# Norm chains with one-tile operands, and where GpSimd's norm products run, in a two-layer decoder trunk

## The chip, the cores and the metric

The kernel runs on one core of a Trainium2 chip. The metric is the device time of one execution in microseconds (us), shown as the median of three runs. PE is TensorE (the matrix engine), DVE is VectorE, ACT is ScalarE, POOL is GpSimd, and SP only issues transfers. Every engine runs its own list of instructions in order and waits on semaphores for the others.

## What is computed

The reference is a trunk of two layers over 512 tokens of width 1024, all in float32:

```python
for l in range(2):
    h = mixing(x)                        # x @ w_in, four kinds of causal heads, RMS norm per head, @ w_out
    x = layernorm(alpha * x + h, ln1_g[l], ln1_b[l])
    m = hier_moe(x)                      # logits -> group (top 1) -> two experts in it, gates
                                         # per expert: (silu(x @ w1) * (x @ w3)) @ w2
    x = layernorm(alpha * x + m, ln2_g[l], ln2_b[l])
def layernorm(x, g, b):
    mu, var = mean(x), mean((x - mu) ** 2)
    return (x - mu) * rsqrt(var + 1e-5) * g + b
```

The mixer has stick-breaking (sb), forgetting (fox), latent (mla) and dilated (d0, d1, d2) heads. There are 16 experts of hidden width 512.

## The kernel before

The 512 tokens are four tiles of 128, one token on a partition. SBUF is handed out by hand: 42 "pages" of 128x1024 floats and 12 small "pg" pages; PSUM is 8 "bank"s; "st" and "nst" are small columns of one value per token. Weights come through one queue on SP, page by page. A weight that isn't used raw is split in two: ACT writes a rounded high part and DVE the rest (`TENSOR_TENSOR page<-page,page 128x1024`, called a lo below), and PE multiplies by both.

All engine orders are written when the kernel is built, by the planner `Plan` (line 88). Each piece of work is a strand that says what it needs (banks, pages, events, an engine). The planner keeps a clock for each engine, costs each instruction, and takes next the strand that could start first, by priority. What it emits is the order of each engine on the chip. All instructions go through one helper, so every row of the trace names line L250, and pieces are told apart by tile names and shapes.

The first norm of a layer (`first_norm`, `first_norm_out`, lines 1464 to 1550) comes after w_out, tile 3 first and tile 0 last. DVE takes the statistics, ACT a first value y of the root, and DVE refines it with `rs_newton` (line 405) and makes m = -mean*y: one tensor_tensor and three scalar_tensor_tensor on 128x1 columns of SBUF. Then ACT writes z = x*y + m. From z, `first_norm_affine` makes z*g + b: POOL for tiles 3, 2, 1 in products of 1024 columns and for the last 384 columns of tile 0; DVE has 640 columns of tile 0 in steps of 160. The logits of the router (`wg`) wait on the same y and m. `route` picks group and experts and writes `asb`, PE counts with it, `posm` gives each token its place in each expert's list, and a list `xidx` comes out; `gslot` are the gates. The expert of rank 0 doesn't wait for a gather: PE selects its rows from SBUF.

The expert loop (line 2263) does for expert e: w1, the first half of w3, then expert e-1's second weights w2 (`hidden_T`, then four quarters), then the rest of w3 and the product silu(h1)*h3. Expert 0 uses its weights raw in float32, others use the split. `use` and `fill` convert weights some places ahead of the one in use.

The second norm of layer 0 (`second_norm`, `second_norm_out`, lines 1591 to 1680) runs from PSUM: statistics and the same chain on DVE, ACT writes z, PE transposes it for the next layer's projections, and POOL makes z*g + b for the residual in two products of 1024 columns per tile and stores it (`xd`). In the last layer ACT writes z from the banks and `affine_by` makes z*g + b on both engines: DVE the first 384, 512, 640, 768 columns of tiles 0 to 3, in steps of 384.

## Time and profile before

| | us |
|---|---|
| median of three runs | 1615.7 (1611.23 to 1615.98) |
| profiled execution, its own time | 1619.65 |
| span of its trace | 1617.7 |
| busy PE, DVE, ACT, POOL | 1436.7, 1099.8, 890.5, 368.7 |

The span has, in this order: attention of layer 0 to about 416 us, its first norm and router to 457, its experts to 765, the second norm and the projections of layer 1 to about 870, the rest of its attention to 1208, its router to 1252, its experts to 1595, and the last norm and the stores to the end. PE is busy most of the time, so what counts is where it stands still and for whom. A bracket at the end of a row of the timeline gives the engine's idle time before that row and what ended it; a row with xN is N instructions that follow each other, and the time is of all of them.

### The profile page before, as it was taken

The numbers are of one execution on the slowest core, as the hardware profiler recorded it, in microseconds if no ns is written. First come the engines' busy times: TensorE is split into PE (matmuls) and PEld (weight loads), VectorE is DVE, ScalarE is ACT, GpSimd is POOL, SyncE is SP. The second block draws the span as 40 slices with busy tenths as digits, with TensorE's granted clock in tenths as the row PEclk, the third lists the DMA queues.
The fourth block names the chain that finished last, engine by engine and source line by source line (L and its number), as shares of the span: only waits on it lengthen the run. The fifth ranks groups of instructions, "written<-read, shape, count | busy, mean of one in ns | idle before, by whom it ended". The sixth has DMA issues, their size and how long they took to land. (4 is left out here: it accounts for less than half of the span.)

```text
span 1617.7 us, 22596 instructions
## 1 busy us (share of the span) xinstructions
PE 1436.7 (89%) x7620; PEld 1164.3 (72%) x7620; DVE 1099.8 (68%) x1967; ACT 890.5 (55%) x1695; POOL 368.7 (23%) x388
## 2 busy tenths in 40 slices
PE   7999989989799999888799998989786999899674
PEld 7988878878666767655699987878666667666453
DVE  4745575476686889977774546654658779898667
ACT  5435454434346888775543534545424477887553
POOL 2511120240412224311421112002204213323002
PEclk9989999999899999988798999989887999999797
DMA  9201211263579999985330102204545799999813
GB/s 266 65 1 41 89 42 40 83 232 143 195 264 319 370 379 356 377 318 173 105 90 23 40 27 92 65 21 134 213 166 195 263 355 382 386 347 385 302 34 130
DMA packets 120700, 303.54 MB, mean 188 GB/s; under 512 B 21982, under 2 KB 45230, under 8 KB 120568
## 3 DMA queue, kind: packets, MB, share of 16 engines
q1 hardware_dynamic: 106936, 269.74, 45.9%
q0 software_dynamic: 12448, 32.11, 7.1%
q8 instruction: 64, 1.05, 0.3%
q14 instruction: 68, 0.56, 0.1%
q10 hardware_dynamic: 1184, 0.08, 0.1%
HBM read 284.14 MB, written 27.33 MB: 193 GB/s over the span
## 5 line engine op out<-in xcount | busy, mean ns | idle before, releaser
L250 PE MATMUL bank<-page,page 128*128 128x512 f32 (+5 forms) x4480 | 983.1, 371 | 62.1 <-DVE page L250 35.0
L250 PEld LDWEIGHTS bank<-page,page 128*128 128x128 f32 (+2 forms) x4480 | 760.6, 203 | 197.9 <-DVE page L250 55.2
L250 DVE TENSOR_TENSOR page<-page,page 128x1024 fp32r<-128x1024 f32 (+3 forms) x470 | 525.7, 1163 | 154.3 <-ACT page L250 140.8
L250 ACT ACTIVATE page<-page 128x1024 fp32r<-128x1024 f32 (+3 forms) x454 | 436.2, 1021 | 49.1 <-DMA page<-in_w_in_dram 11.8
L250 PE MATMUL bank<-page,pg 128*128 128x64 f32 (+1 forms) x1360 | 317.0, 375 | 32.3 <-ACT page L250 14.7
L250 PEld LDWEIGHTS bank<-page,pg 128*128 128x128 f32 x1360 | 227.0, 202 | 115.1 <-issue 37.8
L250 ACT ACTIVATE page<-bank 64x512 fp32r<-64x512 f32 (+8 forms) x255 | 122.1, 506 | 197.1 <-PE bank L250 135.7
L250 ACT ACTIVATE pg<-bank 128x256 f32<-128x256 f32 (+6 forms) x223 | 101.4, 469 | 223.5 <-PE bank L250 221.6
L250 POOL DMA_INDIRECT yd<-page,xidx x30 | 67.5, 2249 | 403.3 <-ACT page L250 165.9
L250 DVE TENSOR_TENSOR page<-bank,page 128x512 fp32r<-128x512 f32 (+4 forms) x142 | 79.9, 599 | 65.9 <-ACT page L250 65.7
L250 POOL TENSOR_TENSOR page<-pg,pg 128x256 f32<-128x256 f32 (+1 forms) x56 | 51.1, 928 | 270.0 <-DVE pg L250 211.5
L250 PE MATMUL bank<-cid,pg 128*128 128x128 f32 (+2 forms) x500 | 84.2, 286 | 29.4 <-ACT pg L250 19.4
L250 POOL TENSOR_TENSOR page<-page,page 128x1024 f32<-128x1024 f32 (+4 forms) x32 | 63.1, 1971 | 153.4 <-ACT page L250 104.7
L250 PE MATMUL bank<-cid,page 128*128 128x128 f32 (+1 forms) x608 | 86.5, 280 | 10.5 <-DVE page L250 5.4
L250 PEld LDWEIGHTS bank<-cid,pg 128*128 128x128 f32 (+2 forms) x500 | 58.7, 147 | 46.2 <-ACT pg L250 25.1
L250 PEld LDWEIGHTS bank<-cid,page 128*128 128x128 f32 (+1 forms) x608 | 71.6, 143 | 24.9 <-DVE page L250 7.7
L250 ACT ACTIVATE pg<-pg 128x256 f32<-128x256 f32 (+5 forms) x146 | 68.6, 477 | 22.3 <-DVE pg L250 18.4
L250 POOL DMA_INDIRECT page<-x1d,xidx x30 | 54.5, 1818 | 42.4 <-DVE e_slots L250 17.9
L250 POOL CAST page<-page 64x512 fp32r<-64x512 f32 x48 | 29.9, 623 | 136.3 <-ACT page L250 102.8
L250 DVE COPY pg<-bank 128x256 f32<-128x256 f32 (+3 forms) x73 | 35.2, 484 | 28.4 <-PE bank L250 28.2
L250 DVE TENSOR_TENSOR pg<-bank,pg 64x512 f32<-64x512 f32 (+6 forms) x81 | 44.8, 559 | 11.9 <-ACT pg L250 10.8
L250 POOL MEMSET page<- 128x1024 f32 (+1 forms) x34 | 44.7, 1319 | 1.8 <-DVE page L250 1.8
(217 smaller groups left out, 974.4 us busy)
## 6 DMA issues: line engine op xcount, KB each, us to landing
page<-in_w_dram SPq DMA_DIRECT2D x396, 512.0 KB, 10.9
page<-in_w_in_dram SPq DMA_DIRECT2D x64, 512.0 KB, 4.1
page<-in_w_out_dram SPq DMA_DIRECT2D x16, 512.0 KB, 4.1
x1d<-page SPq DMA_DIRECT2D x8, 512.0 KB, 2.8
yd<-page SPq DMA_DIRECT2D x8, 512.0 KB, 5.1
page<-yd SPq DMA_DIRECT2D x8, 512.0 KB, 7.0
scr<-pg POOLq DMA_DIRECT2D x16, 132.0 KB, 2.0
pg<-scr POOLq DMA_DIRECT2D x16, 132.0 KB, 4.5
```

What stands on the lines that cost most here:

```text
L250: r = f(*args, **kw)
```

## The change

1. `norm_stats`: `rs_newton` and the m after it are replaced by four tensor_scalar, in which y, v and the mean come as scalars of a partition, so that each has one tensor operand.
2. First norm: tiles 3 and 2 are done on POOL, tiles 1 and 0 on DVE, all in steps of 256 columns (16 products on each engine); DVE's wait for the event `chosen`, which `route` sets when the lists have been started.
3. Second norm of layer 0: POOL's eight products wait for the event `d1q` of the next layer's projections.
4. Last norm: DVE takes (bank - mean)*g from PSUM while ACT makes y, then x*y + b on the first 256, 256, 384, 640 columns; for the rest ACT multiplies by y and POOL adds b. The norm by ACT from the banks is gone.
5. Expert 0's w2 is loaded and used at the end of its own turn, not in expert 1's; expert 1's rows are taken up before its third quarter (`ROWS_AT`).
6. The last expert's w2 is not converted before the product of its hidden layer (`held_at`).
7. The planner lets a DVE tensor_tensor with two SBUF tensors wait for a running POOL tensor_tensor of that kind in its own clocks, which alters the order of other strands.

```diff
+    def newton_1(y, v, t):
+        nc.vector.tensor_scalar(t, y, y, None, op0=OP.mult)
+        nc.vector.tensor_scalar(t, t, -0.5, v, op0=OP.mult, op1=OP.mult)
+        nc.vector.tensor_scalar(y, t, 1.5, y, op0=OP.add, op1=OP.mult)
...
         yield Need(eng="ACT")
         rs_act(y, v)
+        if between:
+            yield from between(mvt[:, 0:1])
         yield Need(eng="DVE")
-        rs_newton(y, v, st(1))
-        nc.vector.scalar_tensor_tensor(m, mvt[:, 0:1], -1.0, y, op0=OP.mult, op1=OP.mult)
+        newton_1(y, v, st(1))
+        nc.vector.tensor_scalar(m, mvt[:, 0:1], -1.0, y, op0=OP.mult, op1=OP.mult)
...
-            plan.spawn(first_norm_affine(nc.gpsimd, t, z, c0, D, D, left), first=1)
-            if c0:
-                plan.spawn(first_norm_affine(nc.vector, t, z, 0, c0, 160, left), first=1)
+            if t in LN1_DVE:                                   # (0, 1)
+                plan.spawn(first_norm_affine(nc.vector, t, z, LN1_STEP, [ev["xT", t], ev["chosen"]]), first=8)
+            else:
+                plan.spawn(first_norm_affine(nc.gpsimd, t, z, LN1_STEP, [ev["xT", t]]), first=1)
...
     def second_norm_out(l, t, z, last, stored):
-        yield Need()
-        affine(t, z, *last.gb, 0, 0)
+        for a in range(0, D, LN2_STEP):                        # 1024
+            for w, op in zip(last.gb, (OP.mult, OP.add)):
+                yield Need(evs=[ev[LN2_AT]], eng="POOL")       # "d1q"
+                c = slice(a, a + LN2_STEP)
+                nc.gpsimd.tensor_tensor(z[:, c], z[:, c], w[:, c], op=op)
...
+                    nc.vector.scalar_tensor_tensor(z[:, c], bs[n], mean, last.gb[0][:, c], op0=OP.subtract, op1=OP.mult)
...
+    def out_sum_1(t, b, cut, y, left):
+        yield Need(eng="DVE")
+        nc.vector.scalar_tensor_tensor(xt[t][:, 0:cut], xt[t][:, 0:cut], y, b[:, 0:cut], op0=OP.mult, op1=OP.add)
+        left()
+    def out_sum_2(t, b, cut, y, left):
+        yield Need(eng="ACT")
+        nc.scalar.activation(xt[t][:, cut:], xt[t][:, cut:], AF.Copy, scale=y)
+        yield Need(eng="POOL")
+        nc.gpsimd.tensor_tensor(xt[t][:, cut:], xt[t][:, cut:], b[:, cut:], op=OP.add)
+        left()
...
-            if e > 0:
+            if e > 1:
                 moe_q[l, e - 1, "w2"] = [block(w2, l, e - 1, q) for q in range(4)]
...
+            if e == 0:
+                moe_q[l, 0, "w2"] = [block(w2, l, 0, q) for q in range(4)]
...
+            if e == 0:
+                ht = hidden_T(prev, "raw" if 0 in RAW_2 else KIND[0])
+                ys = [bank([128, 512]) for _ in range(2)]
+                for j in range(4):
+                    if j == ROWS_AT:                           # 2
+                        next_rows(0)
+                    i = moe_q[l, 0, "w2"][j]
+                    quarter2(ys, ht, use(i), j)
+                    used(i)
+                rel(*ht)
+                scatter(gated(ys, gslot[:, 0:1], KIND[0]), xidx[:, 0:1], SLOTS[0])
+            if e == NE - 1:
+                held_at[0] = moe_q[l, NE - 1, "w2"][3]
+                fill()
...
+                two = "tensor_tensor" in op and ins[0].space != PSUM and ins[-1].space != PSUM
+                if two and eng == "DVE":
+                    for a, b in self.pool_tt:
+                        if a <= start < b:
+                            start = b
```

On DVE, behind the router of layer 0: `xidx` and `gslot` come from the last small matmul, the rows after them rank the experts, and the four 128x1024 rows are los of weights. Before:

```order
L250 TENSOR_SCALAR xidx<-bank_4722 128x16
L250 COPY gslot<-bank_4722 128x16
L250 TENSOR_TENSOR pg_4730<-st_119 128x256
L250 TENSOR_REDUCE st_125<-pg_4730 128x16
L250 TENSOR_TENSOR pg_4730<-st_125,rank_at 128x256
L250 TENSOR_TENSOR pg_4731<-pg_4730,eidx 128x256
L250 TENSOR_REDUCE st_126<-pg_4731 128x16
L250 CAST order<-st_126 128x16
L250 TENSOR_TENSOR pg_4731<-pg_4730,n_slots 128x256
L250 TENSOR_REDUCE e_slots<-pg_4731 128x16
L250 TENSOR_TENSOR page_4752<-page_4180,page_4750 128x1024
L250 TENSOR_TENSOR page_4758<-page_4208,page_4756 128x1024
```

The same place now, from `xidx` on; page_3762 and page_3760 are tiles 1 and 0 of the first norm:

```order
L261 TENSOR_SCALAR xidx<-bank_4711 128x16
L261 COPY gslot<-bank_4711 128x16
L261 TENSOR_TENSOR page_3762<-page_3762,page_4185 128x256
L261 TENSOR_TENSOR pg_4720<-st_119 128x256
L261 TENSOR_TENSOR page_3760<-page_4564,page_4184 128x256
L261 TENSOR_REDUCE st_125<-pg_4720 128x16
L261 TENSOR_TENSOR page_3760<-page_3760,page_4185 128x256
L261 TENSOR_TENSOR pg_4720<-st_125,rank_at 128x256
L261 TENSOR_TENSOR page_3760<-page_4564,page_4184 128x256
L261 TENSOR_TENSOR pg_4721<-pg_4720,eidx 128x256
L261 TENSOR_TENSOR page_3760<-page_3760,page_4185 128x256
L261 TENSOR_REDUCE st_126<-pg_4721 128x16
```

Nine products of the first norm stand among the ranks behind `xidx`; seven more are ahead of it. The eleven rows of `further_table`, three los, and then expert 0's product follow:

```order
L261 TENSOR_TENSOR page_4777<-rk,iota 128x576
L261 TENSOR_TENSOR page_4777<-page_4777,sx_130 128x576
L261 TENSOR_TENSOR page_4780<-page_4777,e_151 128x576
L261 TENSOR_REDUCE extab<-page_4780 128x9
L261 TENSOR_TENSOR page_4780<-page_4777,sx_129 128x576
L261 TENSOR_REDUCE extab<-page_4780 128x9
L261 CAST ntab<-extab 128x9
L261 TENSOR_TENSOR page_4793<-page_4297,page_4791 128x1024
L261 TENSOR_TENSOR page_4797<-page_4299,page_4795 128x1024
L261 TENSOR_TENSOR page_4821<-page_4307,page_4819 128x1024
L261 TENSOR_TENSOR pg_4771<-pg_4771,bank_4786 128x512
```

Here `further_table` (rk, extab, ntab) is a table for experts with many tokens, and pg_4771 is expert 0's silu(h1)*h3. Before, that product stood behind `further_table`, five los and the halves of expert 1's rows, and PE had expert 1's w1 ahead of the first matmul that needs it; now the next matmuls on PE after w3 are those of `hidden_T` on it.

On POOL, at the second norm of layer 0: before, the two products of a tile and its store stand at once behind the loads (page_9407, 9409, 9411 and 9413 are the tiles, page_9509 and 9510 g and b).

```order
L250 TENSOR_TENSOR page_9407<-page_9407,page_9509 128x1024
L250 TENSOR_TENSOR page_9407<-page_9407,page_9510 128x1024
L250 DMA xd_298<-page_9407 128x1024
L250 TENSOR_TENSOR page_9409<-page_9409,page_9509 128x1024
L250 TENSOR_TENSOR page_9409<-page_9409,page_9510 128x1024
L250 DMA xd_298<-page_9409 128x1024
```

Now they stand behind and among the adds that finish the rotary embedding of the dilated heads' q and k (128x256, from pg pages); page_9422, 9424, 9426, 9428 are the tiles:

```order
L261 TENSOR_TENSOR page_10002<-pg_10194,pg_10195 128x256
L261 TENSOR_TENSOR page_9422<-page_9422,page_9524 128x1024
L261 TENSOR_TENSOR page_10206<-pg_10279,pg_10280 128x256
L261 TENSOR_TENSOR page_10206<-pg_10310,pg_10311 128x256
L261 TENSOR_TENSOR page_10206<-pg_10325,pg_10326 128x256
L261 TENSOR_TENSOR page_10206<-pg_10367,pg_10368 128x256
L261 TENSOR_TENSOR page_9424<-page_9424,page_9524 128x1024
L261 TENSOR_TENSOR page_9426<-page_9426,page_9524 128x1024
L261 TENSOR_TENSOR page_9428<-page_9428,page_9524 128x1024
L261 TENSOR_TENSOR page_9422<-page_9422,page_9525 128x1024
L261 CAST page_10499<-page_10499 64x512
```

The products moved from the norm itself to the stage that makes the dilated heads' q and k; three more adds follow among the casts of sb's k.

On DVE, the last rows of the program, the last norm's tiles 2 and 3. Before:

```order
L250 TENSOR_SCALAR st_74<-st_73 128x1
L250 TENSOR_TENSOR page_18732<-page_18732,page_18739 128x384
L250 TENSOR_TENSOR page_18732<-page_18732,page_18739 128x128
L250 TENSOR_TENSOR page_18734<-page_18734,page_18738 128x384
L250 TENSOR_TENSOR page_18734<-page_18734,page_18738 128x256
L250 TENSOR_TENSOR st_75<-nst 128x1
L250 SCALAR_TENSOR_TENSOR st_75<-st_75,st_74 128x1
L250 SCALAR_TENSOR_TENSOR nst<-st_75,nst 128x1
L250 SCALAR_TENSOR_TENSOR nst<-st_73,nst 128x1
L250 TENSOR_TENSOR page_18734<-page_18734,page_18739 128x384
L250 TENSOR_TENSOR page_18734<-page_18734,page_18739 128x256
L250 TENSOR_TENSOR page_18736<-page_18736,page_18738 128x384 x2
```

And now:

```order
L261 TENSOR_SCALAR st_74<-nst 128x1
L261 TENSOR_SCALAR st_74<-st_74,st_71 128x1
L261 TENSOR_SCALAR nst<-st_74,nst 128x1
L261 TENSOR_SCALAR nst<-st_70,nst 128x1
L261 SCALAR_TENSOR_TENSOR page_18766<-bank_18894,st_72,page_18768 128x512
L261 SCALAR_TENSOR_TENSOR page_18764<-page_18764,nst,page_18769 128x384
L261 SCALAR_TENSOR_TENSOR page_18766<-bank_18895,st_72,page_18768 128x512
L261 TENSOR_SCALAR st_75<-nst 128x1
L261 TENSOR_SCALAR st_75<-st_75,st_73 128x1
L261 TENSOR_SCALAR nst<-st_75,nst 128x1
L261 TENSOR_SCALAR nst<-st_72,nst 128x1
L261 SCALAR_TENSOR_TENSOR page_18766<-page_18766,nst,page_18769 128x640
```

The products by g now read a bank and stand ahead of the chain of their tile; one sum of 640 columns is left behind the last chain, where four products of 384 stood.

## Rows read from the trace of the kernel before

**Rows 1.** Page, part 1: busy us (share of the span) xinstructions.

```profile
PE 1436.7 (89%) x7620; PEld 1164.3 (72%) x7620; DVE 1099.8 (68%) x1967; ACT 890.5 (55%) x1695; POOL 368.7 (23%) x388
```

**Rows 2.** Timeline, layer 0's router: start us, us, engine, operation, count [idle before <-releaser].

```profile
419.52 4.82 POOL L250 TENSOR_TENSOR page<-page,page 128x1024 f32<-128x1024 f32 x2 [31.02 <-ACT page L250]
...
422.41 0.15 DVE L250 TENSOR_SCALAR st<-st 128x1 f32<-128x1 f32 x1
...
431.42 3.60 PE L250 MATMUL bank<-wg,page 128*128 128x20 f32 x16
...
433.73 4.77 POOL L250 TENSOR_TENSOR page<-page,page 128x1024 f32<-128x1024 f32 x2 [1.56 <-ACT page L250]
...
434.01 2.09 DVE L250 TENSOR_TENSOR st<-nst 128x1 f32<-128x1 f32 x1 [0.91 <-ACT nst L250]
...
436.33 2.38 DVE L250 SCALAR_TENSOR_TENSOR nst<-st,nst 128x1 f32<-128x1 f32 x2
...
439.65 0.24 DVE L250 TENSOR_TENSOR sel<-lgt,top 128x80 f32<-128x80 f32 x1
...
440.47 0.97 DVE L250 TENSOR_TENSOR sel<-sel,toptmp 128x80 f32<-128x80 f32 x1
...
444.79 0.19 PE L250 MATMUL bank<-asb,tri 128*128 128x16 bf16 x1 [9.77 <-DVE asb L250]
```

**Rows 3.** Timeline, layer 1: from the list to expert 0's product.

```profile
1252.53 10.55 PE L250 MATMUL bank<-page,page 128*128 128x512 f32 x24
1252.71 0.17 DVE L250 TENSOR_SCALAR xidx<-bank 128x16 int32<-128x16 f32 x1 [0.38 <-PE bank L250]
...
1255.86 0.42 DVE L250 TENSOR_REDUCE e_slots<-pg 128x16 f32<-128x256 f32 x1
...
1256.19 4.62 DVE L250 TENSOR_TENSOR page<-page,page 128x1024 fp32r<-128x1024 f32 x4
...
1260.73 0.22 DVE L250 TENSOR_TENSOR sx<-e_slots,c 128x64 f32<-128x64 f32 x1
...
1266.26 0.16 DVE L250 CAST ntab<-extab 128x9 int32<-128x9 f32 x1
```

**Rows 4.** Timeline, last expert of layer 1, then last norm.

```profile
1578.01 1.11 PE L250 MATMUL bank<-cid,pg 128*128 128x128 f32 x4 [3.48 <-DVE pg L250]
...
1595.64 1.48 DVE L250 TENSOR_TENSOR st<-nst 128x1 f32<-128x1 f32 x1
...
1606.69 4.20 DVE L250 TENSOR_TENSOR page<-page,page 128x384 f32<-128x384 f32 x6
```

**Rows 5.** Timeline, second norm of layer 0.

```profile
772.65 1.41 DVE L250 TENSOR_TENSOR st<-nst 128x1 f32<-128x1 f32 x1
...
783.00 5.30 POOL L250 TENSOR_TENSOR page<-page,page 128x1024 f32<-128x1024 f32 x2 [5.67 <-ACT page L250]
783.71 5.67 DVE L250 TENSOR_TENSOR page<-page,page 128x656 fp32r<-128x656 f32 x2 [0.52 <-ACT page L250]
...
811.62 2.93 DVE L250 TENSOR_TENSOR page<-page,page 128x256 fp32r<-128x256 f32 x4
```

**Rows 6.** Waits of PE, 735 to 815: engine, line, waited for: us, times, longest.

```profile
PE bank L250 <- DVE page L250: 13.2, 8, 3.2
```

**Rows 7.** Windows: us, busy (x) of PE, PEld, DVE, ACT, POOL, PEclk, DMA share, GB/s.

```profile
825.00:840.00 15.00, 15.00 (x128) 15.00 (x128) 13.15 (x30) 7.88 (x11) 3.44 (x4) 1.00 0.21 63
1155.00:1185.00 30.00, 17.28 (x74) 12.15 (x72) 22.09 (x92) 13.59 (x49) 4.74 (x8) 0.66 0.30 102
1252.00:1318.00 66.00, 65.61 (x241) 41.47 (x242) 46.09 (x60) 36.88 (x47) 13.43 (x10) 1.00 0.83 296
1320.00:1400.00 80.00, 76.52 (x335) 58.16 (x333) 71.45 (x77) 65.83 (x85) 22.55 (x15) 0.98 1.02 379
```

**Rows 8.** Timeline of PE: ends of the attention of layers 0 and 1.

```profile
352.37 1.12 PE L250 MATMUL bank<-cid,pg 128*128 128x128 f32 x4 [5.60 <-ACT pg L250]
...
1159.38 0.69 PE L250 MATMUL bank<-page,page 128*128 128x128 f32 x2 [4.13 <-DVE page L250]
```

More of the change, by code (lines that the diff above doesn't have):

```diff
@@ L44 @@
 ROWS = 3
+ROWS_AT = 2
 LOOK_AHEAD = (2, 10)
@@ L64 @@
 EX_PAGES = 0
-LN1_DVE = 640
+LN1_DVE = (0, 1)
+LN1_STEP = 256
+LN2_STEP = 1024
+LN2_AT = "d1q"
 XT_DVE = (2, 2)
-OUT_DVE = (384, 512, 640, 768)
-OUT_STEP = 384
+OUT_DVE = (256, 256, 384, 640)
 SPLIT_X = 3
@@ L94, in __init__ @@
             self.books, self.floor, self.moves = {}, {}, []
+            self.pool_tt = deque(maxlen=64)
             self.end = self.now = 0.0
@@ L193, in note @@
             else:
+                two = "tensor_tensor" in op and ins[0].space != PSUM and ins[-1].space != PSUM
[3 more added lines that the diff above has]
+                            start = b
                 end, by = start + self.cost(eng, op, outs, ins), eng
+                if two and eng == "POOL":
+                    self.pool_tt.append((start, end))
                 self.clock[eng] = end
@@ L684, in xT_tile, with norm_stats @@
             rel(b)
-    def norm_stats(t, eps=LN_EPS):
+    def norm_stats(t, eps=LN_EPS, between=None):
         mvt, v = st(2), st(1)
@@ L830, in attention @@
             on(u, NT if U[u].kind == "tok" else 2)
-        for n in ("mla", "forget", "krope", "wfox", "fc"):
+        for n in ("mla", "forget", "krope", "wfox", "fc", "chosen"):
             on(n)
@@ L1603, in second_norm, with centred @@
         yield Need(eng="DVE")
+        z = xt[t]
+        if final:
+            def centred(mean):
+                for n in range(2):
+                    c = slice(n * 512, (n + 1) * 512)
+                    yield Need(eng="DVE")
+                    nc.vector.scalar_tensor_tensor(z[:, c], bs[n], mean, last.gb[0][:, c], op0=OP.subtract, op1=OP.mult)
+                rel(*bs)
+            y, m = yield from norm_stats(t, LN_EPS / ALPHA ** 2, centred)
+            cut = OUT_DVE[t]
+            left = countdown(2, lambda: plan.spawn(second_norm_end(t, last), first=t))
+            plan.spawn(out_sum_2(t, last.gb[1], cut, y, left), first=t)
+            plan.spawn(out_sum_1(t, last.gb[1], cut, y, left), first=t)
+            return
         y, m = yield from norm_stats(t, LN_EPS / ALPHA ** 2)
         yield Need(eng="ACT")
-        z = xt[t]
         for n in range(2):
@@ L1609, in second_norm @@
         rel(*bs)
-        if final:
-            cut = OUT_DVE[t]
-            left = countdown(2, lambda: plan.spawn(second_norm_end(t, last), first=t))
-            for eng, a, b in ((nc.vector, 0, cut), (nc.gpsimd, cut, D)):
-                plan.spawn(affine_by(eng, t, last.gb, a, b, left), first=t)
-            return
         yield Need(pages=1, banks=2)
@@ L1623, in second_norm @@
         plan.spawn(second_norm_out(l, t, z, last, stored[t]))
-    def affine_by(eng, t, gb, c0, c1, left):
-        step = OUT_STEP if eng.name == "DVE" else c1 - c0
-        for w, op in zip(gb, (OP.mult, OP.add)):
-            for a in range(c0, c1, step):
-                yield Need(eng=eng.name)
-                c = slice(a, min(c1, a + step))
-                eng.tensor_tensor(xt[t][:, c], xt[t][:, c], w[:, c], op=op)
+    def out_sum_1(t, b, cut, y, left):
+        yield Need(eng="DVE")
+        nc.vector.scalar_tensor_tensor(xt[t][:, 0:cut], xt[t][:, 0:cut], y, b[:, 0:cut], op0=OP.mult, op1=OP.add)
[5 more added lines that the diff above has]
+        nc.gpsimd.tensor_tensor(xt[t][:, cut:], xt[t][:, cut:], b[:, cut:], op=OP.add)
         left()
@@ L1766, in route @@
             fetched.set()
+            ev["chosen"].set()
             yield dve
@@ L2261, in use_13, with next_rows @@
                 used(i)
+        def next_rows(e):
+            xs_[e + 1] = rows_T(rows.pop(e + 1), KIND[e + 1])
+            if e + ROWS < NE:
+                rows[e + ROWS] = fetch(SLOTS[e + ROWS], xidx[:, e + ROWS:e + ROWS + 1])
         for e in range(NE + 1):
@@ L2278, in trunk @@
                 h3 = bank([128, 512])
-            ht = hidden_T(prev, "raw" if e - 1 in RAW_2 else KIND[e - 1]) if e else None
+            ht = hidden_T(prev, "raw" if e - 1 in RAW_2 else KIND[e - 1]) if e > 1 else None
             if e < NE:
@@ L2283, in trunk @@
                 use_13(e, "w3", h3, range(2))
-            if e:
+            if e > 1:
                 ys = [bank([128, 512]) for _ in range(2)]
@@ L2310, in trunk @@
                 break
-            if e + 1 < NE:
-                xs_[e + 1] = rows_T(rows.pop(e + 1), KIND[e + 1])
-                if e + ROWS < NE:
-                    rows[e + ROWS] = fetch(SLOTS[e + ROWS], xidx[:, e + ROWS:e + ROWS + 1])
+            if 0 < e < NE - 1:
+                next_rows(e)
             if e == EX_RUN:
```

32 lines of the change are left out of this document (11 added, 21 removed).

## The prediction, on record before the changed kernel ran

> **What bounds the kernel now.** I read the page's busy shares first: PE is busy 1436.7 us of the span, far ahead of the others [rows 1]. So the time is PE's work plus the stretches in which PE stands still or runs slowly. The windows show both kinds of stage [rows 7]: with the experts PE is busy 65.61 of 66 us and 76.52 of 80, with the projections of layer 1 15.00 of 15; but at the end of layer 1's attention only 17.28 of 30, at a granted clock of 0.66. What is worth anything are such holes, and I looked at the timeline of each that the change touches.
>
> The hole at the router shows the mechanism on which most of the change turns [rows 2]. A 128x1 product of DVE takes 2.09 us, and the pair behind it 2.38, although each handles one value per partition. Both end where one of POOL's 1024-column products ends: POOL runs 433.73 to 438.50, in two of 2.4 us, and DVE's run ends at 436.10 and 438.71. These DVE instructions have two tensors from SBUF. A tensor_scalar with one, inside POOL's 419.52 to 424.34, took 0.15. So a DVE instruction with two SBUF operands waits for POOL's running product, one with a single SBUF operand does not.
>
> The Trainium skill says the same ("SBUF — State Buffer", section "Who interferes with whom"): DVE's second input comes through ports shared with GpSimd, held for a whole instruction. But the same section, with "VectorE: DVE Perf Modes", section "Mode 2×_2P", also lets tensor_scalar hold the shared pair, where source and destination lie in SBUF and the shape allows it. By that rule the new chains could wait as well; the 0.15 us row speaks against it, for immediate scalars. It is rival 3.
>
> **The change part by part** (against the profiled execution, 1619.65 us with a span of 1617.7; that is 3.95 above the median of 1615.7, and I carry the sum over to the median unchanged).
>
> *Router, both layers.* Four tensor_scalar at 0.15 us are 0.6 for a chain that took from 434.01 to 438.71 [rows 2]: about 4 less. Nothing else is late until PE's last logit matmuls, which end at 431.42 + 3.60 = 435.02 whatever DVE does; the logits need them too, so the choice starts near 435.5 in place of 439.4: -3.9. In the choice itself two products run into POOL's 384-column pair; one shows 0.97 us against 0.24 for its like, so two cost 1.5. In the new order POOL's part is tiles 3 and 2 alone, which come first, and it is idle by then: -1.5. Against that, seven products of tiles 1 and 0 stand ahead of `xidx` on DVE. A 256-column operation is 0.42 us [rows 3], seven are 2.9; DVE waits for PE there in part, so 0 to 2.9, I take +0.9. PE waited 9.77 us for `asb` [rows 2], so all of it is on its path. Sum -4.5 per layer (bounds -1.5 and -5.4), -9 for two; layer 1's rows repeat layer 0's.
>
> *Expert 0's w2 at once.* From `xidx` PE has w1 and w3 of expert 0: 32 float32 matmuls at 10.55/24 = 0.44, so 14.1 us from 1252.53, to 1266.6 [rows 3]. Then comes `hidden_T`, which needs the product. DVE after `xidx` (1252.71): gates and ranks to 1256.28 (3.4), now with nine products of 0.42 between (3.8), `further_table` 1260.73 to 1266.42 (5.7), three los at 4.62/4 = 1.16 (3.5), then the product (about 0.7): 17.1, so it ends near 1269.9. PE waits 3.3, then some 0.6 more for ACT's copy of the transposed tile, which other matmuls covered before. +3.9 per layer (0 if the rows of `further_table` and the los are shorter or start earlier, 6 if the nine also meet POOL), +7.8. Today nothing waits there (65.61 of 66 busy [rows 7]). The rest of the edit moves 16 matmuls and a scatter earlier and is worth nothing: PE does the same work.
>
> *Last expert.* PE waits 3.48 us for a product that stands behind two los of 1.16 [rows 4]. The product goes ahead of them: up to -2.3 per layer; but the los are then late for w2's first quarter. I take -1 each (0 to -2.3): -2.
>
> *Second norm of layer 0.* Seven DVE rows between 772.65 and 811.62 are longer than their kind: 1.41 for 0.15, 5.67 for about 2, 2.93 for about 1.5 [rows 5]; together 12.9 us. In that stretch PE waited 13.2 us for DVE's pages [rows 6]. With POOL idle they go, and ACT's writing of z is next, which already ends a part of PE's waits. I take two thirds: -8 (0 to -11). The chain itself would not wait without POOL, so here the two edits count once.
>
> *The products moved to layer 1's projections.* Eight of 4.82/2 = 2.41 us are 19.3 us of POOL among DVE's adds, los and POOL's own rope adds. DVE is busy 13.15 of 15 us there and PE never waits [rows 7]. A DVE product with two SBUF operands that meets one waits about half of it; the order has slack of a tile or so, so most is hidden: +2 (0 to +19). Their `xd` stores come later, and are read only a layer later. The four tiles and g, b keep six of 42 pages longer, in a stage with a DMA share of 0.21 [rows 7]: nothing.
>
> *Planner.* It reorders the attention of both layers. In layer 0 the end shows one wait of 5.60 us and little else [rows 8]: -2.5 (±3). In layer 1 the last 30 us have 12.7 idle, the largest 4.13 for a DVE page [rows 7, 8], and what runs is slow at 0.66. The new order puts the small sums that merge the dilated heads ahead of fox's scores, as in layer 0, where the hole is smaller, and spreads the filler matmuls over the end in place of one block after it. I take -9: half of the idle and a third of what the clock costs (17.28 us at 0.66 are 11.4 at 1, so 5.9). Bounds -14 and +8.
>
> *The end.* A 128x1 product waits 1.48 us there, and DVE has 4.20 us of sums left in its last row, to 1610.89 [rows 4]. After: one sum of 640 columns (about 0.85) behind the last chain, the products by g from the banks, which PE has finished. By the durations of the shown kinds DVE ends near 1607.1: -3.8 (-2 to -5). POOL's part stays at 256 to 768 columns, one product in place of two.
>
> *Experts between.* PE is the bound to 1318, and later the DMA is as well: a share of 1.02 at 379 GB/s [rows 7]. Loads start as pages come free, pages come free as PE goes on, so an earlier start shifts all of it.
>
> Sum: -2.5 - 9 + 7.8 - 2 - 8 + 2 - 9 - 3.8 = -24.5; 1615.7 - 24.5 = **1591**.
>
> **Rivals.**
>
> 1. *The planner's order brings nothing in layer 1.* Its costs are not the chip's; the holes of 0.4 to 4 us there are chains between ACT, DVE and PE, and any order has them. Then -9 turns to +5 and -2.5 to 0: -8, 1608. For it: the planner also wrote today's order, with this hole. Against it: layer 0 has the better order, and the smaller hole.
> 2. *The loads are the bound.* If the DMA, full from 1318 on, doesn't start earlier, what is gained or lost ahead of the experts is swallowed: -2.5 - 9 + 7.8 - 9 = -12.7 of the sum goes, and 1604 is left. For it: a share of 1.02. Against it: PE is still busy 76.52 of 80.
> 3. *The chains still wait.* If a tensor_scalar with scalars from SBUF columns waits for POOL like the old form, 3.9 per layer is lost: 1599. For it, the form isn't in the trace; against it, the 0.15 us row.
> 4. *The moved products cost more than they did, slower than before.* The place is layer 1's dilated q and k. If PE loses each of the eight in full, that is 19.3 us, and the holes lower the clock as in 1155 to 1185: 30 us of PE work at 0.66 take 15 more. +34 in place of +2: -24.5 + 32 = +7.5, 1623. It decides from 24.5 us above my +2. For it: DVE is the busiest helper there; against it: each product meets one DVE instruction, and PE has matmuls queued.
>
> **How the numbers follow.** My forecast holds with 0.54 (its own range 1578 to 1604), rival 1 with 0.18, rival 2 with 0.12, rival 3 with 0.05, rival 4 with 0.06; 0.05 is left for gains beyond my bounds or a mishap not named. 0.3%, 4.9 us, is about what a measurement of this kernel can tell from no change. Faster by more: 0.54, 0.05, most of rivals 1 and 2 (0.20) and half of the rest: 0.80. Within: the upper ends of rivals 1 and 2: 0.12. Slower: rival 4 and some of the rest: 0.08. The range runs from 1575 (the LN2, planner and end terms at their good bounds lie below) to 1614, which takes in rivals 1 to 3.
>
> **What would show it.** In the changed trace: 128x1 tensor_scalar rows of 0.15 us during POOL's products (rival 3 if they take 1 to 2); PE's wait for `asb` at 5 us in place of 9.8; a new wait of PE for a DVE pg of 3 to 4 us about 14 us after `xidx`; no DVE row over 2 us for one product in the second norm; PE at 15 of 15 still in the projections of layer 1 (rival 4 if it falls below 13); PE over 22 of the last 30 us of layer 1's attention (rival 1 if not). I am wrong above all if the planner's order makes layer 1's end longer, which no row of before can exclude.

## The result, and the profile of the changed kernel

The changed kernel takes 1599.24 us in the median of 6 runs (1596.7 to 1608.6), the kernel before 1614.68 us beside it; the ratio is 0.9915, with a 95% interval of 0.9892 to 0.9938. By the ratio that is 13.7 us faster (the medians lie 15.4 apart), in the range and in the direction of the forecast, and a little over half of its 24.5. One execution of the kernel of experiment 2 took 4735.87 us, three times the others, and is left out of its median as of its ratio. The profiled execution took 1600.47 us with a span of 1598.7, 19.0 less than the span of before. Where these 19.0 come from is read from both traces at the same instructions on DVE: the first aggregate of the statistics of a norm, the list `xidx`, the cast of `xidx` before the last scatter, and the first row on `lat_ss`, the latents' statistics. All stretches are differences of such start times; the end is the span less the last of them.

| stretch, us | before | changed | difference | forecast |
|---|---|---|---|---|
| attention of layer 0, to its first norm | 415.9 | 421.5 | +5.6 | -2.5 |
| router of layer 0, to `xidx` | 41.8 | 36.2 | -5.6 | -4.5 |
| experts of layer 0, to the last scatter | 285.5 | 295.9 | +10.4 | +3.9 |
| last expert, to the second norm | 24.5 | 24.9 | +0.4 | -1 |
| second norm, to `lat_ss` | 55.0 | 42.2 | -12.8 | -8 |
| rest of layer 1's attention | 387.8 | 375.2 | -12.6 | -9 + 2 |
| router of layer 1 | 42.1 | 36.4 | -5.7 | -4.5 |
| experts of layer 1 | 321.3 | 326.3 | +5.0 | +3.9 |
| last expert | 16.2 | 15.6 | -0.6 | -1 |
| last norm and stores | 27.5 | 24.5 | -3.0 | -3.8 |

The sum is near the forecast only because large errors of both signs cancel. The page of the changed kernel, part 1, answers to [rows 1]: PE has 10 us more of busy time for the same 7620 matmuls in a shorter span, DVE 12 less.

```profile
PE 1446.7 (90%) x7620; PEld 1164.4 (73%) x7620; DVE 1087.6 (68%) x1981; ACT 888.1 (56%) x1689; POOL 354.0 (22%) x400
```

The router of layer 0 in the timeline of the changed kernel (start, us, engine, operation, count, idle time before) answers to [rows 2].

```profile
433.69 5.99 POOL L261 TENSOR_TENSOR page<-page,page 128x256 f32<-128x256 f32 x8 [2.36 <-ACT page L261]
...
435.19 0.20 DVE L261 TENSOR_SCALAR st<-nst 128x1 f32<-128x1 f32 x1
...
438.68 0.21 DVE L261 TENSOR_SCALAR st<-nst 128x1 f32<-128x1 f32 x1 [1.49 <-ACT nst L261]
...
440.56 0.24 DVE L261 TENSOR_TENSOR sel<-lgt,top 128x80 f32<-128x80 f32 x1
...
443.75 0.19 PE L261 MATMUL bank<-asb,tri 128*128 128x16 bf16 x1 [3.93 <-DVE asb L261]
```

A tensor_scalar of the new chain takes 0.20 us inside POOL's products of 433.69 to 439.68, where the old form took 2.09. The products of the choice meet no POOL and take 0.24. PE waits 3.93 us for `asb`, not 9.77.

Behind the list of layer 0, the same stretch as [rows 3] (those are of layer 1):

```profile
457.67 0.17 DVE L261 TENSOR_SCALAR xidx<-bank 128x16 int32<-128x16 f32 x1
...
469.07 3.49 DVE L261 TENSOR_TENSOR page<-page,page 128x1024 fp32r<-128x1024 f32 x3
...
472.48 0.68 DVE L261 TENSOR_TENSOR pg<-pg,bank 128x512 f32<-128x512 f32 x1
...
473.21 0.66 PE L261 MATMUL bank<-cid,pg 128*128 128x128 f32 x4 [1.75 <-DVE pg L261]
...
474.56 5.40 PE L261 MATMUL bank<-page,pg 128*128 128x512 f32 x8 [0.69 <-ACT pg L261]
...
480.54 1.10 PE L261 MATMUL bank<-cid,page 128*128 128x128 f32 x8 [0.59 <-DMA page<-x1d,xidx]
```

Expert 0's product starts 14.8 us behind `xidx` (forecast: 16.4), and PE waits for it 1.75, then 0.69 for ACT's copy and 0.59 for the rows of expert 1: 3.0 in place of 3.9. What the forecast had not: eight float32 matmuls right behind the waits take 5.40 us, 0.68 each, where those ahead of them take 0.44 (13.98 for 32, from 457.48). The window of 473 to 478 (us, busy time and count of PE, PEld, DVE, ACT, POOL, then PEclk, DMA share, GB/s) shows the clock that was granted:

```profile
473.00:478.00 5.00, 4.10 (x9) 1.93 (x10) 2.52 (x3) 2.49 (x3) 4.28 (x4) 0.69 0.74 258
```

That is only the start of what these experts lose. Their whole stretch, before and then changed:

```profile
457.69:743.23 285.54, 267.04 (x1096) 187.71 (x1096) 236.96 (x278) 211.52 (x272) 73.84 (x44) 0.98 0.90 327
457.67:753.56 295.89, 272.86 (x1096) 190.06 (x1096) 239.65 (x286) 213.47 (x273) 73.80 (x44) 0.96 0.90 326
```

Of the 10.4 us, PE stands still for 4.5 (23.0 in place of 18.5) and takes 5.8 more for the same 1096 matmuls, at a granted clock of 0.96 in place of 0.98.

The second norm, as windows of both kernels, first before and then changed:

```profile
767.74:822.78 55.04, 39.68 (x243) 36.72 (x242) 38.67 (x70) 30.57 (x82) 24.47 (x15) 0.78 0.35 111
```

```profile
778.44:820.66 42.22, 36.53 (x253) 33.28 (x252) 27.01 (x71) 30.35 (x82) 1.08 (x2) 0.92 0.31 88
830.00:875.00 45.00, 44.72 (x337) 42.09 (x336) 31.82 (x59) 15.95 (x30) 31.35 (x27) 1.00 0.15 50
```

POOL is busy 1.08 us there in place of 24.47, and DVE does the same work in 27.01 us of busy time in place of 38.67: that is the waiting of DVE. The stretch is 12.8 us shorter: PE stands still for 9.7 less (15.4, then 5.7), and its matmuls take 3.2 less, at a granted clock of 0.92 in place of 0.78. Where POOL's eight products now run, 830 to 875, PE is busy 44.72 us of 45: there they cost it next to nothing.

The last expert answers to [rows 4]; PE waits for its product and for the w2 behind it. Changed:

```profile
1560.31 0.66 PE L261 MATMUL bank<-cid,pg 128*128 128x128 f32 x4 [1.24 <-DVE pg L261]
...
1562.60 0.50 PE L261 MATMUL bank<-page,pg 128*128 128x512 f32 x1 [1.63 <-ACT page L261]
1563.86 8.20 PE L261 MATMUL bank<-page,pg 128*128 128x512 f32 x28 [0.76 <-DVE page L261]
1572.26 4.83 PE L261 MATMUL bank<-page,pg 128*128 128x512 f32 x19 [0.20 <-DVE page L261]
```

And before, behind the wait of 3.48:

```profile
1579.81 13.28 PE L250 MATMUL bank<-page,pg 128*128 128x512 f32 x48 [0.69 <-ACT pg L250]
```

The waits are 1.24, 1.63, 0.76 and 0.20 us against 3.48 and 0.69: as feared, the converted w2 is now late, and of the possible 2.3 us only 0.3 are gained in waits. In the last norm, DVE's last sum (answers to 1606.69 in [rows 4]):

```profile
1589.40 0.88 DVE L261 SCALAR_TENSOR_TENSOR page<-page,nst,page 128x640 f32<-128x640 f32 x1
1589.96 1.16 POOL L261 TENSOR_TENSOR page<-page,page 128x384 f32<-128x384 f32 x1 [0.62 <-ACT page L261]
```

DVE ends 16.1 us behind the first aggregate of its statistics (1574.18), before it was 20.7 (1590.22 to 1610.89). The span ends 3.0 us earlier, the rest is lost behind POOL and the last store.

### The profile page after: what moved, and what is told of

It is laid out like the page before. It is cut to its first block, busy times and chain, and to the rows that moved or that the text cites. A ratio compares the mean times of both kernels' runs of the same rounds, so it can differ in the third digit from the quotient of the medians.

```text
span 1598.7 us, 22565 instructions
## 1 busy us (share of the span) xinstructions
PE 1446.7 (90%) x7620; PEld 1164.4 (73%) x7620; DVE 1087.6 (68%) x1981; ACT 888.1 (56%) x1689; POOL 354.0 (22%) x400
## 5 line engine op out<-in xcount | busy, mean ns | idle before, releaser
L261 PE MATMUL bank<-page,page 128*128 128x512 f32 (+5 forms) x4480 | 970.3, 367 | 41.9 <-DVE page L261 22.3
L261 PEld LDWEIGHTS bank<-page,page 128*128 128x128 f32 (+2 forms) x4480 | 751.4, 200 | 178.2 <-DVE page L261 43.4
L261 DVE TENSOR_TENSOR page<-page,page 128x1024 fp32r<-128x1024 f32 (+2 forms) x472 | 520.0, 1146 | 154.1 <-ACT page L261 146.7
L261 PE MATMUL bank<-page,pg 128*128 128x64 f32 (+1 forms) x1360 | 336.3, 392 | 40.7 <-ACT page L261 20.2
L261 PEld LDWEIGHTS bank<-page,pg 128*128 128x128 f32 x1360 | 237.7, 212 | 129.9 <-issue 37.5
L261 ACT ACTIVATE page<-bank 128x256 f32<-128x256 f32 (+6 forms) x256 | 122.4, 506 | 196.1 <-PE bank L261 127.4
L261 ACT ACTIVATE pg<-bank 128x256 f32<-128x256 f32 (+5 forms) x222 | 101.3, 471 | 222.0 <-PE bank L261 220.2
L261 PE MATMUL bank<-cid,pg 128*128 128x128 f32 (+2 forms) x500 | 87.0, 290 | 27.5 <-ACT pg L261 17.2
L261 POOL TENSOR_TENSOR page<-page,page 128x256 f32<-128x256 f32 (+4 forms) x44 | 48.9, 1125 | 80.2 <-ACT page L261 78.9
L261 DVE TENSOR_TENSOR pg<-bank,pg 64x512 f32<-64x512 f32 (+6 forms) x81 | 44.9, 560 | 10.5 <-ACT pg L261 9.4
L261 ACT ACTIVATE page<-bank,gslot 128x512 f32<-128x512 f32 (+1 forms) x36 | 24.6, 687 | 40.3 <-PE bank L261 37.7
```

What stands on the lines that cost most here:

```text
L261: r = f(*args, **kw)
```

## Experiments

Each ratio is to the kernel before, on the same chip.

**1. Expert 0's w2 back in expert 1's turn** (on the changed kernel).

```diff
-            if e > 1:
+            if e > 0:
                 moe_q[l, e - 1, "w2"] = [block(w2, l, e - 1, q) for q in range(4)]
...
-            if e == 0:
-                moe_q[l, 0, "w2"] = [block(w2, l, 0, q) for q in range(4)]
...                                  # use and rows_T(1) likewise as before
```

> The changed kernel with expert 0's second weights again loaded and used in expert 1's turn; all else as changed. In the changed kernel the time from the list xidx to the last expert's scatter is 10.3 us longer than before in layer 0 and 5.0 in layer 1. Theory A (loads): SP's queue holds the stores of the first norm's tiles 1 and 0 ahead of the weights' loads, and these stores now wait for DVE's products, so the loads start 9 to 12 us later; then this kernel loses PE's waits of about 3.0 us per layer behind expert 0, but the loads stay late and both stretches stay at least 3 us longer than before: 0 to 3 us per layer gained, 1594 to 1599. Theory B (the stall): PE's wait for expert 0's product is the cost; then both stretches come back to within 2 us of before, 1584 to 1590.

Measured: 1611.82 us in 10 runs, ratio 0.9975 (0.9949 to 1.0001): slower than the changed kernel by some 10 by the ratios, 12.6 by the medians. Both theories fail. The waits of PE from `xidx` to the last scatter in layer 0 (engine, line, waited for: us, times, longest):

```profile
PE bank L261 <- DMA page<-x1d,xidx: 10.9, 1, 10.9
PE bank L261 <- DVE page L261: 7.9, 11, 1.3
```

One wait of 10.9 us for the gathered rows of expert 1, 10.0 in layer 1; PE waits for no pg of DVE any more beyond 0.7. The rows are gathered from x1d, and x1d of tiles 1 and 0 is stored after DVE's products, which the change put behind `chosen`. The last store of x1d and the first gather, before (`xidx` at 457.69) and then here (`xidx` at 449.57):

```profile
455.93 0.33 SPq L250 DMA_DIRECT2D x1d<-page  x1
...
461.05 1.12 POOL L250 DMA_INDIRECT page<-x1d,xidx  x1 [16.86 <-DVE pg L250]
```

```profile
456.65 0.33 SPq L261 DMA_DIRECT2D x1d<-page  x1
...
464.76 1.12 POOL L261 DMA_INDIRECT page<-x1d,xidx  x1 [31.57 <-DMA x1d<-page]
```

The store was issued 1.8 us ahead of `xidx` and now 7.1 behind it; the gather started 3.4 behind it and now starts 15.2 behind it, when the store has landed. PE's order in the experts is that of before here, and they take 296.5 and 332.9 us, 10.9 and 11.6 more than before, about as much as these two waits for late rows. In the changed kernel 16 more float32 matmuls (eight of w3, eight of w2) stand ahead of the first matmul on these rows, and the experts take 0.6 and 6.6 less than here. So w2 at once covers a part of another edit's cost. What else makes the 10 us isn't seen: this profile is among the shorter runs of its kernel (1606.23 us), and its other large differences to the changed kernel lie in attention with the same orders (-8.3 in layer 0, +6.0 in layer 1).

**2. The stores of these tiles on ACT's queue** (on the changed kernel; orders of PE, DVE and POOL identical).

```diff
-            nc.sync.dma_start(x1d[l][t * 128:(t + 1) * 128, :], xp...)
+            (nc.scalar if t in LN1_DVE else nc.sync).dma_start(x1d[l][t * 128:(t + 1) * 128, :], xp...)
...                                  # yd likewise
```

> The changed kernel with the stores x1d and yd of the first norm's tiles 1 and 0 issued on ACT's queue in place of SP's; the orders of PE, DVE and POOL are the same. Theory A (loads): the loads behind xidx start 8 to 12 us earlier on SP, and the stretch from xidx to the last expert's scatter shortens by 4 to 8 us in layer 0 and 3 to 5 in layer 1: 1586 to 1592. Theory B (the stall behind expert 0): the stretches don't change by more than 2 us: 1597 to 1601. If ACT's own work waits behind the stores, a third outcome: a longer router, slower by 1 to 3 us.

Measured: 1589.85 us in 3 runs, ratio 0.984 (0.9811 to 0.9868). The time is that of theory A, the mechanism isn't. The experts take 293.0 and 325.6 us, 2.9 and 0.8 less than changed, not 4 to 8 and 3 to 5. SP's issues behind the router of layer 0, of the kernel before, the changed one and this one:

```profile
448.47 2.78 SPq L250 DMA_DIRECT2D page<-in_w_dram  x4
...
462.94 34.93 SPq L250 DMA_DIRECT2D page<-in_w_dram  x21
```

```profile
459.47 0.32 SPq L261 DMA_DIRECT2D x1d<-page  x1
...
460.43 3.93 SPq L261 DMA_DIRECT2D page<-in_w_dram  x4
...
472.24 28.04 SPq L261 DMA_DIRECT2D page<-in_w_dram  x15
```

```profile
440.99 58.30 SPq L261 DMA_DIRECT2D page<-in_w_dram  x20
```

In the changed kernel the loads do stand behind the stores (459.47), 9 to 12 us later than before. But with the stores out of the way, 20 loads are still spread over 58 us: they wait for pages. Of SP's waits from 440 to 500 us, 29.7 end with an instruction of DVE on a page and 12.0 with one of PE. About half of the gain is in the experts (3.6 of the 6.0 us between the two spans); the rest is in stretches with the same orders, so this run doesn't settle what else it gained.

**3. Without the planner's rule** (on the changed kernel).

```diff
-                if two and eng == "DVE":
+                if False:
```

> The changed kernel without the planner's new rule on DVE and POOL products with two SBUF tensors; all else as changed. In the changed kernel layer 0's attention ends 5.5 us later than before with the same sum of PE's waits (29 and 30 us). Theory: the rule's order costs these 5.5 us in layer 0, and brings about 9 us in layer 1: layer 0's attention ends near 416 again, layer 1's stretch from its second norm's first statistics to the router's (417.4 us now, 442.9 before) grows by 5 to 12: 1598 to 1606. Rival: the rule brings nothing in layer 1, the whole gain there is the second norm's products moved: 1592 to 1595.

Measured: 1588.65 us in 4 runs, ratio 0.9828 (0.9792 to 0.9864): faster than the changed kernel by 10.6 by the medians, 14 by the ratios. Layer 0's attention has the order of before again and ends at 411.2; the rest of layer 1's attention takes 370.8 us. Against these gains the experts of layer 1 take 330.3, 4.0 more than in the changed kernel in the same order. The rule costs in both layers; not even the rival went so far.

**4. The second norm's products at once again** (on the changed kernel).

```diff
-                yield Need(evs=[ev[LN2_AT]], eng="POOL")
+                yield Need(eng="POOL")
```

> The changed kernel with the second norm's eight products of layer 0 on POOL at once, as before, in place of waiting for d1q. Theory: the DVE stalls of 12.9 us come back but for the chains (tensor_scalar), so about 6 to 9 us of them, and PE's waits in the second norm with them; layer 1's stretch (417.4 us now) grows by 6 to 12: 1605 to 1611. Rival: the gain of layer 1's stretch is the planner's order alone: within 3 us of the changed kernel.

Measured: 1619.7 us in 10 runs, ratio 1.0022 (0.9995 to 1.0049): 20 us slower than the changed kernel by the medians, 17 by the ratios, more than the theory said. The second norm takes 52.7 us (10.5 more), and the rest of layer 1's attention 387.8 (12.6 more), as before to the tenth. The last 70 us of that attention, in the windows of before, of changed and of this run:

```profile
1140.60:1210.60 70.00, 55.98 (x275) 44.77 (x274) 40.70 (x143) 20.43 (x70) 8.77 (x14) 0.85 0.44 156
```

```profile
1125.87:1195.87 70.00, 62.78 (x326) 52.02 (x325) 37.01 (x110) 23.31 (x78) 2.15 (x5) 0.85 0.44 163
```

```profile
1150.63:1220.63 70.00, 55.98 (x274) 44.80 (x274) 40.70 (x143) 20.43 (x70) 8.77 (x14) 0.85 0.43 157
```

This run repeats before (PE 55.98 of 70, DVE 40.70, POOL 8.77), although it has the rule. So the better end of layer 1's attention comes with the moved products, by which the planner writes another order there, and not with the rule. What PE waits for in that whole stretch shows where most of it lies; its largest item, before and then changed:

```profile
PE bank L250 <- DVE page L250: 12.9, 11, 4.1
```

```profile
PE bank L261 <- DVE page L261: 3.2, 3, 1.6
```

All of PE's waits there add up to 28.2 us before, 27.9 in this run and 17.3 in the changed kernel.

**5. That move alone** (on the kernel before).

```diff
-        affine(t, z, *last.gb, 0, 0)
+        for w, op in zip(last.gb, (OP.mult, OP.add)):
+            yield Need(evs=[ev["d1q"]], eng="POOL")
+            nc.gpsimd.tensor_tensor(z, z, w, op=op)
```

> The kernel before with one edit: the second norm's eight products of layer 0 on POOL wait for d1q. Old chains, old first norm, old planner, old end. Theory (the move alone is the main gain, in two places): the second norm's stretch to the latents' statistics (55.0 us before, 42.2 changed, 52.7 with the products put back) falls to about 43 to 45, and the planner writes another end of layer 1's attention with it, so that the stretch from there to the router (387.8 before) falls to 371 to 381: 1592 to 1599. Rival: the gain needs the new chains or the rule: 1605 to 1613.

Measured: 1584.34 us in 4 runs, ratio 0.9809 (0.9767 to 0.9852), better than the theory and than the whole change. The second norm takes 40.1 us with the old chains, the rest of the attention 369.7; both routers, the experts and the end are as before (41.7, 285.3, 41.6, 322.5, 27.5). Of the 37.5 us between the two spans, 5.6 lie in layer 0's attention, whose order is the same. The second norm, and the last 70 us of layer 1's attention:

```profile
762.13:802.26 40.13, 34.32 (x244) 31.55 (x243) 26.27 (x70) 30.38 (x82) 1.08 (x2) 0.91 0.33 93
1101.91:1171.91 70.00, 62.01 (x352) 52.41 (x351) 41.27 (x112) 26.40 (x83) 8.45 (x10) 0.95 0.52 192
```

**6. The rule alone** (on the kernel before).

```diff
...                                  # two: a tensor_tensor with both tensors in SBUF
+                if two and eng == "DVE":
+                    for a, b in self.pool_tt:
+                        if a <= start < b:
+                            start = b
...                                  # POOL's products are noted in pool_tt
```

> The kernel before with one edit: the planner's rule on products with two SBUF tensors. Theory (the rule costs in layer 0's attention and brings nothing in layer 1): layer 0's attention ends at 418 to 422 in place of 415.9, layer 1's stretches stay within 3 us: 1616 to 1624. Rival (layer 0's end varies by itself by 5 us, the rule does nothing): within 3 us of before, 1612 to 1617.

Measured: 1618.88 us in 10 runs, ratio 1.0019 (0.9995 to 1.0043): the interval holds no change. Layer 0's attention took 423.5 us in its profile. One profile tells little here, since the stretch varies, so I take all of them: with the rule's order (changed and experiments 1, 2, 4, 6, 7, 8) 413.2 to 427.8, mean 422.1 of 7; with the order of before (before and 3, 5, 9, 10) 410.3 to 415.9, mean 413.3 of 5. That is 8.8 us more with the rule's order. It is rather too much, since the profiled executions of the seven lie some 4 us above the medians of their kernels on average and those of the five some 1. The windows of this stretch in this run and in experiment 5:

```profile
0.00:423.49 423.49, 394.06 (x2402) 347.69 (x2403) 238.19 (x529) 190.49 (x502) 79.73 (x162) 0.94 0.32 102
```

```profile
0.00:410.32 410.32, 380.91 (x2402) 337.09 (x2403) 236.53 (x529) 189.86 (x502) 82.86 (x162) 0.97 0.34 105
```

PE stands still 29.4 us in both. It is busy 394.06 and 380.91 us with the same 2402 matmuls, at a granted clock of 0.94 and 0.97.

**7. All first-norm products on POOL, in steps of 256** (on the changed kernel; PE's order identical).

```diff
-LN1_DVE = (0, 1)
+LN1_DVE = ()
```

> The changed kernel with the first norm's products of tiles 1 and 0 on POOL too, in steps of 256; PE's order is the same. Theory (late rows): with DVE's products away from xidx the stores x1d come earlier, PE's waits for expert 0's product and for the gathered rows (3.0 us, and 1.9 of lowered clock behind them) go, and the stretches behind xidx shorten by 4 to 6 us in each layer; the route's products of two SBUF tensors meet POOL's, +1 to +4 per router: 1590 to 1597. Rival: the router loses as much as the experts gain: 1598 to 1602.

Measured: 1597.06 us in 4 runs, ratio 0.9883 (0.9854 to 0.9912). The experts come back by 7.0 and 3.1 us (288.9 and 323.2, still 3.4 and 1.9 above before), the routers lose 3.2 and 3.0 (39.5 and 39.4). Both halves of the theory are seen; the sum is between it and its rival, and can't be told from the changed kernel.

**8. The old chains** (on the changed kernel; PE's order identical).

```diff
-        newton_1(y, v, st(1))
-        nc.vector.tensor_scalar(m, mvt[:, 0:1], -1.0, y, ...)
+        rs_newton(y, v, st(1))
+        nc.vector.scalar_tensor_tensor(m, mvt[:, 0:1], -1.0, y, ...)
```

> The changed kernel with the old chain of the norms (one tensor_tensor and three scalar_tensor_tensor of 128x1) in all norms; PE's order is the same. Theory (chains with two SBUF tensors wait for POOL): the old chains wait for POOL's products of 256 columns (0.75 us each) in the two routers, 1 to 3 us per layer on the path, nothing in the second norm, where POOL is idle, and 1 to 2 at the end: 1602 to 1607. Rival (the chain's form is worth nothing once POOL's products are short or elsewhere): within 2 us of the changed kernel.

Measured: 1598.29 us in 4 runs, ratio 0.9883 (0.9843 to 0.9922): as the rival said. The routers lose 0.8 and 0.6 us, the second norm takes 40.0. The old chain does wait, but for a product of 0.75 us:

```profile
438.56 0.50 DVE L261 TENSOR_TENSOR st<-nst 128x1 f32<-128x1 f32 x1
...
439.29 1.26 DVE L261 SCALAR_TENSOR_TENSOR nst<-st,nst 128x1 f32<-128x1 f32 x2
```

**9. The new chains alone** (on the kernel before; the four lines of `newton_1` in place of `rs_newton`; orders of PE, ACT and POOL identical).

```diff
-        rs_newton(y, v, st(1))
-        nc.vector.scalar_tensor_tensor(m, mvt[:, 0:1], -1.0, y, ...)
+        t = st(1)
+        nc.vector.tensor_scalar(t, y, y, None, op0=OP.mult)
+        nc.vector.tensor_scalar(t, t, -0.5, v, op0=OP.mult, op1=OP.mult)
+        nc.vector.tensor_scalar(y, t, 1.5, y, op0=OP.add, op1=OP.mult)
+        nc.vector.tensor_scalar(m, mvt[:, 0:1], -1.0, y, op0=OP.mult, op1=OP.mult)
```

> The kernel before with one edit: the chains of the norms as tensor_scalar, POOL's products of 1024 columns where they were. PE, ACT and POOL have the same orders. Theory (the wait goes with the second SBUF operand): 128x1 rows take 0.15 to 0.25 us also during POOL's products; each router shortens by about 3.9 (41.8 and 42.1 before), the second norm by 2 (55.0 before): 1604 to 1608. Rival (POOL's own products come earlier and the next DVE product with two operands waits in the chain's place): routers within 1.5 us: 1612 to 1616.

Measured: 1609.79 us in 12 runs, ratio 0.997 (0.9946 to 0.9994). The routers gain 2.1 and 3.0 us (39.6 and 39.1), the second norm nothing (55.4), the end 2.0: between theory and rival. The timeline shows both:

```profile
430.70 6.80 POOL L250 TENSOR_TENSOR page<-page,page 128x1024 f32<-128x1024 f32 x4 [0.66 <-ACT page L250]
...
430.99 0.21 DVE L250 TENSOR_SCALAR st<-nst 128x1 f32<-128x1 f32 x1 [0.45 <-ACT nst L250]
...
433.75 1.84 DVE L250 TENSOR_TENSOR sel<-lgt,top 128x80 f32<-128x80 f32 x1
...
440.17 0.20 PE L250 MATMUL bank<-asb,tri 128*128 128x16 bf16 x1 [8.04 <-DVE asb L250]
```

The chain runs through POOL's products (0.21), and the first products of the choice, which come 4 us earlier with it, run into them instead: 1.84 us for 0.24. PE still waits 8.04 us for `asb`.

**10. The three edits that paid** (on the kernel before): the new chains, the moved products, the last norm from the banks; the rest as before.

```diff
...                                  # the edits of experiments 5 and 9, and
-            for eng, a, b in ((nc.vector, 0, cut), (nc.gpsimd, cut, D)):
-                plan.spawn(affine_by(eng, t, last.gb, a, b, left), first=t)
+            plan.spawn(out_sum_2(t, last.gb[1], cut, y, left), first=t)
+            plan.spawn(out_sum_1(t, last.gb[1], cut, y, left), first=t)
```

> The kernel before with three of the seven edits: the chains as tensor_scalar, the second norm's products of layer 0 after d1q, and the last norm from the banks; first norm, expert 0, last expert and planner as before. The move alone ran in 1584 us. Theory: the terms add up, routers 38 in place of 41.8 each (-3.9 twice), the end 24.4 in place of 27.5 (-3): 1572 to 1577, the fastest of all. Rival: the routers don't shorten: 1580 to 1583.

Measured: 1579.91 us in 5 runs, ratio 0.9776 (0.9756 to 0.9796): faster than both kernels, and close to the rival's time. The end is 24.1 us, the routers 40.8 each, so of the chains' gain only 1.0 and 1.3 are left there. Of the 1.2 us that layer 0's router takes more than in experiment 9, 0.7 lie ahead of the last chain and 0.4 in the 64 matmuls behind `asb` (10.14 us for 9.72); the row of 1.84 us is the same in both. Against experiment 5 the intervals overlap.

## Why the prediction was right in the time and wrong in its steps

**Right: the mechanism.** A DVE product with two SBUF tensors waits for POOL's running product, a 128x1 tensor_scalar with one doesn't: 0.20 us in place of 2.09, in the changed kernel and in experiment 9. Rival 3 is out. It was also right that POOL's work costs less in the projections than in the norm; rival 4 is out with 44.72 us of PE in 45. Rival 2 is out by experiment 5: its lists come 5.7 and 39.2 us earlier than before, and the experts behind them take as long as before (285.3 and 322.5), so what is gained ahead of them isn't swallowed.

**Routers: the size about right, the term wrongly split.** -5.6 and -5.7 for -4.5. The step gave 3.9 of this to the chains. Experiment 8 gives them 0.8 and 0.6 where POOL's products are short, experiment 9 2.1 and 3.0 where they are long. The place of POOL's products does most of the work, and what the chain gains wanders on to the next product.

**Expert 0 and the first norm: the step that failed.** "+3.9 per layer" priced a wait of 3.3 + 0.6 for w2 at once behind the nine products on DVE, and 3.0 with 1.9 of slower matmuls behind it is near. But taking the edit of w2 away makes the experts 0.6 and 6.6 us longer, not shorter (experiment 1). What failed is the price of another edit, the first norm's products of tiles 1 and 0 on DVE: the prediction counted their time on DVE alone (0.9 in the router, 3.8 ahead of expert 0's product) and put at nothing what is stored behind them. x1d waits for these products, the gather of expert 1's rows for x1d, and PE for the rows: one wait of 10.9 and one of 10.0 us with w2 where it was before, in experts that take 10.9 and 11.6 more (experiment 1). With w2 at once, +10.4 and +5.0 are left of both edits together, and without the products on DVE +3.4 and +1.9 (experiment 7). What w2 at once would cost on the kernel before, by itself, was not run. The stores also hold loads back, by 9 to 12 us, and the share of that isn't settled; "an earlier start shifts all of it" was the reverse of what happened.

**Second norm: too small by half.** -8 and +2 were -12.8 and 0; I had taken two thirds of what DVE waits. PE's waits fell by 9.7, and 3.2 came from matmuls at a higher granted clock, a term that the step didn't have. The 13.2 us of [rows 6] are of 735 to 815; in the norm's own stretch PE waited 11.1 for DVE's pages. Experiment 4 puts 10.5 of the 12.8 on the products' place, experiment 5 all of it (40.1 us with the old chains), experiment 9 nothing on the chains.

**Planner: the right size for the wrong cause.** The -9 for layer 1 measured -12.6, but experiments 4 and 5 tie it to the moved products, which I had priced at their stage alone. Some 11 us of it are PE's waits, 9.7 of these for DVE's pages. The sign named for this came true: the prediction called 1155 to 1185 the last 30 us, which ends 25.6 us ahead of the end, and in the same place counted from the end PE is busy 24.59 us in the changed kernel in place of 17.28. The rule costs: 8.8 us in layer 0 (experiment 6), where I had -2.5, and 8.7 in layer 1 (mean 378.7 of five profiles with rule and move, 370.0 of three with the move alone). Both are of single profiles and add up to more than whole kernels show: 10.6 to 14 us in experiment 3, and 3 (-0.8 to 6.9) in experiment 6, whose rule has no moved products beside it. Neither is a matter of waits, which are alike with and without the rule; PE's busy time differs, with the granted clock, and why this order gets a lower one stays open. Rival 1, the order brings nothing, was the nearer one on the rule. Which change of order in layer 1 makes the 12 to 18 us, that of PE or that of its helpers, was not tried.

**End and last expert.** -3.0 for -3.8, and -0.6 and +0.4 for -1: small, as forecast; the last expert's converted w2 came late, as the step feared.

**Sums in the working.** Three don't follow from their own terms, and none decided anything: the router's worst case is -2.5 and not -1.5; half of 12.7 and a third of 5.9 are 8.3 and not 9; and rival 2 keeps -8 + 2 of the second norm, which lies ahead of layer 1's experts too, so that it should stand at 1610. That 1599 came out near 1591 is luck: the stages miss by up to 8 us, with both signs.

The terms that I priced from single waits (routers, end, last expert) hold within 1.4 us. Those that I took from the order of a planner, or from what stands behind a moved instruction, miss by 5 to 8, but for the experts of layer 1.

## What to carry to other kernels

Move a helper's large products away from the stage in which the engine that has to wait for them is on the critical chain: here that one edit of three lines is worth more than the change of seven parts. When a step moves, follow its stores and their readers, not its own duration alone; an edit that looks like a cost may be the cover for another edit's delay, so take each away alone before judging it. A more faithful cost in a planner needn't give a faster order, and an order with the same sum of waits can still be slower: look at the granted clock too.

## What was not expected of the hardware

With one and the same order, layer 0's attention took from 413.2 to 427.8 us from run to run with the rule (7 profiles) and 410.3 to 415.9 without (5), at granted clocks of 0.92 to 0.97 over the stretch, and with PE standing still 29 to 30 us in each of the twelve. The time goes with the clock: 410.3 us at 0.97, 421.5 at 0.94, 427.8 at 0.92. The matmuls behind a wait of 1.75 and 0.69 us ran at 0.68 us in place of 0.44; the row of experiment 1 that ends a wait of 10.9 us shows eight transposes in 1.97 us, against 1.04 for eight of them before. In the window of these 1.97 us, with PE idle for the 10.9 ahead of it, the granted clock is 0.50, the lower of the two levels (1.2 and 2.4 GHz):

```profile
470.84 1.97 PE L261 MATMUL bank<-cid,page 128*128 128x128 f32 x8 [10.90 <-DMA page<-x1d,xidx]
470.84:472.81 1.97, 1.97 (x9) 1.97 (x10) 0.19 (x1) 0.60 (x1) 0.00 (x0) 0.50 0.71 150
```
